# Low parts of the weights by accumulating transfers, softmax scaling on ScalarE: one decoder layer on one Trainium2 core

## The chip, the cores and the metric

The kernel runs on one NeuronCore of a Trainium2 chip. The metric is the device time of one execution in microseconds (us). The median of three runs before the change is 2506.76 us (2502.85 to 2508.31). The engines are named as in the profile: PE (TensorE, matrix multiplications), ACT (ScalarE), DVE (VectorE), POOL (GpSimd) and SP (SyncE, which issues most transfers). POOL and ACT issue transfers too. Each engine, and each of these queues, works through its instructions in order.

## What is computed

One layer of a hybrid decoder (`D_MODEL` 1024, `SEQ` 2048, 256 memory tokens, feed-forward width 2816), all in 32-bit floats:

```python
for l in range(DEPTH):                      # DEPTH = 1
    h = rmsnorm(x, mix_norm_g[l])
    proj = h @ w_in[l]
    q, k, v, g, u = jnp.split(proj, [R, 2 * R, 3 * R, 4 * R], axis=-1)
    y_ret = jax.nn.silu(g) * head_rmsnorm(retention(q, k, v, positions), ret_gn_g[l])
    y_pool = pool_mixer(u, pool_w[l], pool_scale[l])
    x = x + jnp.concatenate([y_ret, y_pool], axis=-1) @ w_out[l]
    x = x + cross_attn(rmsnorm(x, xa_norm_g[l]), mem_n, xa_wq[l], xa_wkv[l], xa_wo[l])
    x = x + conv_glu_ffn(rmsnorm(x, ffn_norm_g[l]), ffn_w_up[l], ffn_conv_w[l],
                         ffn_conv_b[l], ffn_w_down[l])
return rmsnorm(x, final_norm_g)
```

`cross_attn` takes a softmax over the 256 memory tokens for each of 4 heads.

## The kernel before

**Numbers in two parts.** Every large operand is kept as a pair: a high part, rounded to the matmul's format (`float32r`), and a low part, the rest. `passes` (L239) makes three matmuls of a product: high by high (L241), high by low (L242), low by high (L243). The pairs are made by `split` (L230): ACT copies the source into the high tile, which rounds it (L233, or L236 with a scale), and DVE subtracts that from the source (through the helper `tt`, L216; with a scale through `stt`, L225).

**Weights.** SP loads a raw weight tile of 128x1024 into one of five slots of the tile `R` (`load_tile`, L305). `pairs` splits it in two halves of 128x512, each into one of three slots of the tile `Q`, taken in turn. A slot can be written again when PE has done with the half that was in it. `unit` (L285) is one such weight tile against the 1024 tokens of a block: two halves, for each two column ranges `s` of 512 tokens, four `k` and three passes. It then hands the PSUM tile to an `evac` function. Units are used for the head inputs (three for each of 4 heads), the pool groups (4), the output projection (8, loads at L1536 and L1537) and the projection behind attention (8, from `VWd`), in each of two blocks of 1024 tokens.

**Stages.** For each block: head inputs with retention beside them; pool groups, whose halo columns `phalo` POOL copies (L630, L631); the output projection with the residual; attention; the `VWd` projection with the residual, beside which the first block loads the next block's `x` (`xT`, L524) and the second one begins the feed-forward part. The feed-forward part of both blocks follows, from about 1200 us on; it does not use `unit`. The order within an engine is laid down beforehand by a scheduler, from the program's order and its own estimate of when things are ready; nothing is reordered while it runs.

**Weight sums.** The feed-forward part needs sums of weight blocks. They are made in DRAM during the units and the attention of both blocks (`weight_sums`): SP copies four blocks (L913), and POOL issues four accumulating transfers (L915, L916, L919, L922), where L919 needs the landing of L915, and L922 that of L919. There are 34 such jobs, 136 transfers.

**Attention.** Scores for 128 tokens and two heads come from 24 matmuls. DVE takes the maximum (L871), ACT the exponentials with their sums (L875), DVE the reciprocal (L877) and the product with the exponentials (helper `ts`, L220). PE transposes the result (`turn`, L850) two tiles later. `load_m` (L835) loads and splits the folded key weights of the first two heads, then, during the first eight tiles, those of the other two.

Of the kernel before, what the change touches and what calls it, by code (L numbers as in the profile page):

```python
# [8 lines left out]
F32 = mybir.dt.float32  # L9
F32R = mybir.dt.float32r  # L10
I32 = mybir.dt.int32
AF = mybir.ActivationFunctionType
ALU = mybir.AluOpType
# [8 lines left out]
SUB = 512  # L22
# [97 lines left out]
def trunk(ctx, tc, xT, memT, pos, w_qkgu, w_v, wkv, wqT, wo, wout_r, wout_p, poolT, w_up, w_dn, vecs, consts, outT):  # L120
    nc = tc.nc
    pe, act, dve, pool, sp = nc.tensor, nc.scalar, nc.vector, nc.gpsimd, nc.sync
# [15 lines left out]
    def new_z(dtype):  # L138
        return Arena(cp.tile([P, 8 * T + 4 * EDGE], dtype, tag="Z", name=nm("Z")), 0, 8, T)
# [58 lines left out]
    def mmps():  # L198
        return mmp.tile([P, SUB], F32, tag="mm", name=nm("mm"))
# [6 lines left out]
    def aux():  # L206
        if both[0] and next(turns_) % 3 == 2:
            return single()
        return auxp.tile([P, SUB], F32, tag="aux", name=nm("aux"))

    def small(n=4):
        t = smp.tile([P, 8], F32, tag="sm", name=nm("sm"))
        return t[:, :n]

    def tt(eng, out, a, b, op):
        return eng.tensor_tensor(out=out, in0=a, in1=b, op=op)  # L216

    def ts(eng, out, a, s1, op0, s2=None, op1=None):
        if op1 is None:
            eng.tensor_scalar(out=out, in0=a, scalar1=s1, scalar2=None, op0=op0)  # L220
        else:
            eng.tensor_scalar(out=out, in0=a, scalar1=s1, scalar2=s2, op0=op0, op1=op1)

    def stt(out, a, s, b, op0=ALU.mult, op1=ALU.add):
        dve.scalar_tensor_tensor(out=out, in0=a, scalar=s, in1=b, op0=op0, op1=op1)  # L225
# [4 lines left out]
    def split(src, hi, lo, g=None):  # L230

        if g is None:
            act.activation(hi, src, AF.Copy)  # L233
            tt(dve, lo, src, hi.bitcast(F32), ALU.subtract)
        else:
            act.activation(hi, src, AF.Identity, scale=g)  # L236
            stt(lo, src, g, hi.bitcast(F32), ALU.mult, ALU.subtract)

    def passes(ps, lhs, rhs, start, stop, more=False):  # L239
        (lh, ll), (rh, rl) = lhs, rhs  # L240
        pe.matmul(ps, lh, rh, start=start, stop=False, skip_group_check=more)  # L241
        pe.matmul(ps, lh, rl, start=False, stop=False, skip_group_check=more)  # L242
        pe.matmul(ps, ll, rh, start=False, stop=stop, skip_group_check=more)  # L243

    def new_raw():
        r = raws.take()
        r.free()
        return r.f

    def new_pair():  # L250
        r = prs.take()
        r.free()
        return r.r.rearrange("p (i n) -> p i n", i=2)

    def pairs(raw):

        out = []
        for h in range(2):
            r = raw[h] if isinstance(raw, list) else raw[:, h * SUB : (h + 1) * SUB]
            pr = new_pair()  # L260
            split(r, pr[:, 0], pr[:, 1])
            out.append(pr)
        return out

# [20 lines left out]
    def unit(raw, rhs, evac, order=range(4)):  # L285


        hs = pairs(raw)
        ps = [mmps() for _ in range(NS)]
        for h in range(2):  # L290
            for s in range(NS):
                for j, kk in enumerate(order):
                    k = 4 * h + kk
                    w = [hs[h][:, i, kk * P : (kk + 1) * P] for i in range(2)]
                    passes(ps[s], w, rhs(k, s), h + j == 0, h == 1 and j == 3)
                next(behind[0], None)
                quarter[0] += 1
                if not slow[0] or quarter[0] % 2:
                    next(under[0], None)
                if h == 1:  # L300
                    evac(s, ps[s])
# [520 lines left out]
    def attention(sums, beside, pace):  # L822


        scl, nscl = (smp.tile([P, 8], F32, tag="scl", name=nm("scl"), bufs=2) for _ in range(2))
        room = B.take(2 * KT)
        third = [Region(B, room.first + KT * i, KT) for i in range(2)] + [new_z(F32R).take(KT)]
        prob = [third[1], third[0]]

        def load_m(hp):  # L830

            out = mw[hp]
            for kp in range(KT // 2):
                raw = new_raw()
                fetched[0] = sp.dma_start(raw.rearrange("p (k n) -> p k n", k=2), Md[hp, 2 * kp : 2 * kp + 2].rearrange("k p n -> p k n"))  # L835
                if hp == 0 and kp == 0:

                    out += [(pr[:, 0], pr[:, 1]) for pr in pairs(raw)]
                    yield
                    continue  # L840
                for i in range(2):
                    u = third[2 * hp].r[:, (2 * kp + i) * T : (2 * kp + i + 1) * T]
                    split(raw[:, i * SUB : (i + 1) * SUB], u[:, :SUB], u[:, SUB:])
                    out.append((u[:, :SUB], u[:, SUB:]))
                yield

        def turn(pt, t, e):
            tp = aux()
            for j in range(4):
                pe.transpose(tp[:, j * P : (j + 1) * P], e.f[:, j * P : (j + 1) * P], ident)  # L850
            pt4 = pt.r.rearrange("p (i k t) -> p i k t", i=2, t=T)[:, :, :, t * P : (t + 1) * P]
            split(tp.rearrange("p (k t) -> p k t", k=4), pt4[:, 0], pt4[:, 1])
            e.free()

        mw = [[], []]
        for _ in load_m(0):
            pass
        more_m = load_m(1)
        late = []
        for i in range(2 * KT):  # L860
            hp, t = divmod(i, KT)
            ps = mmps()
            for k in range(KT):
                x2 = [X[:, 2 * k + j, t * P : (t + 1) * P] for j in range(2)]
                passes(ps, x2, mw[hp][k], k == 0, k == KT - 1)
            if i == 0:
                rn, _, _ = norm_tables(sums, wide=False)
                ts(dve, scl, rn, 1.0 / 16.0, ALU.mult)
                ts(dve, nscl, rn, -1.0 / 16.0, ALU.mult)
            mx, sm = small(2), small(2)  # L870
            dve.reduce_max(out=mx, in_=ps.rearrange("p (h m) -> p h m", h=2), axis=AX.X)  # L871
            ts(dve, mx, mx, nscl[:, t : t + 1], ALU.mult)
            e = TT.take()
            for j in range(2):
                act.activation(e.f[:, j * NMEM : (j + 1) * NMEM], ps[:, j * NMEM : (j + 1) * NMEM], AF.Exp,  # L875
                               bias=mx[:, j : j + 1], scale=scl[:, t : t + 1], accum_out=sm[:, j : j + 1])
            dve.reciprocal(sm, sm)  # L877
            for j in range(2):
                ej = e.f[:, j * NMEM : (j + 1) * NMEM]
                ts(dve, ej, ej, sm[:, j : j + 1], ALU.mult)  # L880
            if len(late) == 2:
                turn(*late.pop(0))
            late.append((prob[hp], t, e))
            for _ in range(pace):
                next(under[0], None)
            if i < KT - 2:
                next(more_m, None)
            else:
                for _ in range(pace):
                    next(beside, None)  # L890

        def end():
            for one in late:
                yield turn(*one)

        return prob, end()
# [129 lines left out]
    class Up(Member):  # L1026
# [15 lines left out]
        def evac(self, i, ps):  # L1042
            if i == 0:
                self.gate = self.place()
            elif i == 1:
                self.val = self.place()
            which, q, how = ((0, 0, 0), (1, 1, 0), (0, 1, 0), (0, 0, 1), (1, 1, 1), (0, 1, 1), (1, 0, 0))[i]
            d = body(self.val if which else self.gate)[:, q * SUB : (q + 1) * SUB]
            if how:
                tt(dve, d, d, ps, ALU.add)  # L1050
            else:
                act.activation(d, ps, AF.Copy)
            if i > 4:
                pending.extend(self.conv(i - 5))
# [365 lines left out]
    def norm_tables(s_acc, wide=True, late=False):  # L1420

        rn = rows_norm(s_acc)
        rb, last = [], None
        if wide:
            rb = [TT.take() for _ in range(NS)]
            last = spread(rn, [r.f[:, :SUB] for r in rb], late=late)
        return rn, rb, last
# [71 lines left out]
    for b in range(NB):  # L1499
# [34 lines left out]
        for n in range(KT):  # L1534
            raw = new_raw()
# [32 lines left out]
        for n in range(KT):  # L1568
# [3 lines left out]
            def rhs(k, s):  # L1572
                at = (k % 4) * T + s * SUB
                return tuple(prob[k // 4].r[:, i * 4 * T + at : i * 4 * T + at + SUB] for i in range(2))
# [152 lines left out]
```

## Time and profile before

| | |
|---|---|
| median of three runs | 2506.76 us |
| the profiled execution | 2506.72 us |
| its span, first to last instruction | 2504.9 us |
| mean granted clock of PE | 0.992 |
| PE busy | 2442.7 us |
| DVE busy | 1666.9 us |
| ACT busy | 1216.1 us |
| POOL busy | 652.4 us |
| transfers issued by POOL | 8.9% of the 16 DMA engines' span |

How to read it: the page adds up busy time by engine. Matmuls overlap in it, so a row's mean of one matmul (some 386 ns) is longer than the time from one to the next. In the timeline, a row gives start, duration, engine, line, operation, the tile written and those read, and in brackets how long the engine had been idle and who ended that. In the groups by line, the columns are the total busy time, the mean in ns, and the idle time before with its causes. Names ending in q are an engine's queue that issues transfers.

### The profile page before, as it was taken

The numbers are of one execution on the slowest core, as the hardware profiler recorded it, in microseconds if no ns is written. First come the engines' busy times: TensorE is split into PE (matmuls) and PEld (weight loads), VectorE is DVE, ScalarE is ACT, GpSimd is POOL, SyncE is SP. The second block draws the span as 40 slices with busy tenths as digits, with TensorE's granted clock in tenths as the row PEclk, the third lists the DMA queues.
The fourth block names the chain that finished last, engine by engine and source line by source line (L and its number), as shares of the span: only waits on it lengthen the run. The fifth ranks groups of instructions, "written<-read, shape, count | busy, mean of one in ns | idle before, by whom it ended". The sixth has DMA issues, their size and how long they took to land.

```text
span 2504.9 us, 33172 instructions
## 1 busy us (share of the span) xinstructions
PE 2442.7 (98%) x11390; PEld 2037.7 (81%) x11390; DVE 1666.9 (67%) x2574; ACT 1216.1 (49%) x2163; POOL 652.4 (26%) x579
## 2 busy tenths in 40 slices
PE   6999999999999999999999999999999999999997
PEld 6888887788788888888887888878888887888885
DVE  8646566564635675574678776886677586867875
ACT  6333423343321223434654555665555576666663
POOL 1010122100121120030237352553335154222322
PEclk9999999999999999999999999999999999999998
DMA  8363888715766764366567564755556468768951
GB/s 318 89 168 110 244 191 233 234 40 181 227 152 145 159 158 149 111 221 220 167 205 270 166 203 153 236 192 165 160 160 213 136 220 287 250 185 280 346 164 68
DMA packets 257177, 474.28 MB, mean 189 GB/s; under 512 B 26864, under 2 KB 56176, under 8 KB 257008
## 3 DMA queue, kind: packets, MB, share of 16 engines
q1 hardware_dynamic: 212336, 408.18, 49.0%
q0 software_dynamic: 19584, 34.61, 8.9%
q10 hardware_dynamic: 25088, 29.37, 3.4%
q8 instruction: 89, 1.46, 0.2%
q14 instruction: 80, 0.66, 0.1%
HBM read 370.87 MB, written 170.39 MB: 216 GB/s over the span
## 4 chain that ended last, share of the span: by engine, by line
PE 78%; DMA 8%; DVE 6%; issue 3%; POOL 2%; ACT 2%; SPq 0%; POOLq 0%; ACTq 0%; DVEq 0%
PE mm L241 25%; PE mm L242 24%; PE mm L243 24%; POOL T L216 1%; DVE Z L216 1%; DMA T<-Xd 1%; DVE Z L225 1%; DVE G L216 1%; DMA T<-xT 1%; DVE Q L216 1%; DVE T L216 1%; DMA T<-Gd 1%; POOL Z L216 1%; PE aux L749 1%; DMA R<-VWd 0%
## 5 line engine op out<-in xcount | busy, mean ns | idle before, releaser
L241 PE MATMUL mm<-G,Q 128*128 128x512 f32 (+1 forms) x1888 | 728.1, 386 | 21.8 <-ACT Q L233 11.1
L243 PE MATMUL mm<-G,Q 128*128 128x512 f32 (+1 forms) x1888 | 725.9, 385 | 4.4 <-DVE Q L216 4.2
L242 PE MATMUL mm<-G,Q 128*128 128x512 f32 (+1 forms) x1888 | 725.7, 385 | 0.7 <-DVE G L216 0.7
L241 PE MATMUL mm<-G 128*128 128x512 f32 (+1 forms) x1380 | 532.1, 387 | 10.0 <-DVE Z L216 6.3
L242 PE MATMUL mm<-G 128*128 128x512 f32 (+1 forms) x1380 | 531.7, 386 | 0.0
L243 PE MATMUL mm<-G 128*128 128x512 f32 (+1 forms) x1380 | 531.1, 385 | 0.0
L241 PEld LDWEIGHTS mm<-G,Q 128*128 128x128 f32 x1888 | 357.8, 190 | 91.1 <-ACT Q L233 11.8
L243 PEld LDWEIGHTS mm<-G,Q 128*128 128x128 f32 x1888 | 357.7, 190 | 74.3 <-DVE Q L216 5.9
L242 PEld LDWEIGHTS mm<-G,Q 128*128 128x128 f32 x1888 | 358.0, 190 | 69.4 <-DVE G L216 1.6
L225 DVE SCALAR_TENSOR_TENSOR Z<-Z,vecs 128x1024 f32<-128x1024 f32 x176 | 276.3, 1572 | 153.5 <-ACT Z L1069 145.3
L241 PEld LDWEIGHTS mm<-G 128*128 128x128 f32 x1380 | 260.4, 189 | 64.5 <-DVE Z L216 8.0
L243 PEld LDWEIGHTS mm<-G 128*128 128x128 f32 x1380 | 260.2, 189 | 51.8
L242 PEld LDWEIGHTS mm<-G 128*128 128x128 f32 x1380 | 260.1, 188 | 51.5
L1006 ACT ACTIVATE G<-R 128x512 fp32r<-128x512 f32 (+1 forms) x272 | 166.5, 615 | 197.8 <-PE mm L242 178.6
L216 DVE TENSOR_TENSOR Z<-Z,mm 128x512 f32<-128x512 f32 x284 | 192.8, 679 | 78.2 <-PE mm L243 78.0
L216 DVE TENSOR_TENSOR Q<-R,Q 128x512 fp32r<-128x512 f32 x199 | 148.6, 748 | 143.4 <-ACT Q L233 138.9
L216 POOL TENSOR_TENSOR G<-R,G 128x512 fp32r<-128x512 f32 (+1 forms) x100 | 141.9, 1420 | 376.2 <-ACT G L1006 290.9
L233 ACT ACTIVATE Q<-R 128x512 fp32r<-128x512 f32 x150 | 93.8, 627 | 234.8 <-PE mm L242 187.3
L1006 ACT ACTIVATE Q<-R 128x512 fp32r<-128x512 f32 (+1 forms) x204 | 125.0, 613 | 90.9 <-PE mm L242 73.5
L216 DVE TENSOR_TENSOR G<-R,G 128x512 fp32r<-128x512 f32 (+1 forms) x168 | 131.5, 794 | 46.7 <-ACT G L233 38.0
L216 DVE TENSOR_TENSOR G<-T,G 128x512 fp32r<-128x512 f32 (+1 forms) x168 | 125.4, 758 | 53.9 <-ACT G L955 40.7
L940 ACT ACTIVATE aux<-R 128x512 f32<-128x512 f32 (+1 forms) x184 | 105.8, 576 | 95.8 <-DVE Q L216 52.9
(222 smaller groups left out, 2911.4 us busy)
## 6 DMA issues: line engine op xcount, KB each, us to landing
R<-Ud SPq DMA_DIRECT2D x176, 256.0 KB, 2.7
T<-Gd SPq DMA_DIRECT2D x168, 256.0 KB, 4.1
R<-w_up SPq DMA_DIRECT2D x132, 256.0 KB, 3.1
Gd<-Z SPq DMA_DIRECT2D x110, 256.0 KB, 2.4
Ud<-w_up SPq DMA_DIRECT2D x88, 256.0 KB, 5.9
R<-w_qkgu SPq DMA_DIRECT2D x32, 512.0 KB, 4.4
R<-Dd SPq DMA_DIRECT2D x64, 256.0 KB, 4.0
Gd<-T SPq DMA_DIRECT2D x56, 256.0 KB, 3.1
```

The lines of the kernel that those rows point to most:

```text
L216: return eng.tensor_tensor(out=out, in0=a, in1=b, op=op)
L225: dve.scalar_tensor_tensor(out=out, in0=a, scalar=s, in1=b, op0=op0, op1=op1)
L233: act.activation(hi, src, AF.Copy)
L241: pe.matmul(ps, lh, rh, start=start, stop=False, skip_group_check=more)
L242: pe.matmul(ps, lh, rl, start=False, stop=False, skip_group_check=more)
L243: pe.matmul(ps, ll, rh, start=False, stop=stop, skip_group_check=more)
L749: pe.matmul(col(self.kv, c), col(self.kn.f, c), self.ch(v, c, h * T), start=True, stop=True)
L940: act.activation(t, x, AF.Copy)
L1006: act.activation(p2[:, 0, :w], self.raw[i].f[:, :w], AF.Copy)
```

## The change

In `unit`, and for the second pair of heads in `load_m`, `split` is replaced by `moved`. ACT writes the negated source, rounded, into the low tile, and the rounded source into the high tile. A transfer issued by POOL then adds the source to the low tile. DVE takes no part. `pairs` gets the function as an argument, and its other callers keep `split`. In the softmax, the two products with the reciprocal, 128x256 each, go from DVE to ACT.

```diff
+    def moved(src, hi, lo):
+
+        act.activation(lo, src, AF.Copy, scale=-1.0)
+        act.activation(hi, src, AF.Copy)
+        pool.dma_start(lo.bitcast(F32), src, accum_op=ALU.add)
+
-    def pairs(raw):
+    def pairs(raw, how=split):
...
-            split(r, pr[:, 0], pr[:, 1])
+            how(r, pr[:, 0], pr[:, 1])
...
     def unit(raw, rhs, evac, order=range(4)):
...
-        hs = pairs(raw)
+        hs = pairs(raw, moved)
...
-                    split(raw[:, i * SUB : (i + 1) * SUB], u[:, :SUB], u[:, SUB:])
+                    (moved if hp else split)(raw[:, i * SUB : (i + 1) * SUB], u[:, :SUB], u[:, SUB:])
...
             for j in range(2):
                 ej = e.f[:, j * NMEM : (j + 1) * NMEM]
-                ts(dve, ej, ej, sm[:, j : j + 1], ALU.mult)
+                act.activation(ej, ej, AF.Identity, scale=sm[:, j : j + 1])
```

## The prediction

> **What bounds the kernel now.** I read the page first, then the waits by engine, the groups by line, the DMA issues, the busy time by stage, and last the timelines of the stages that the change touches.
>
> ```profile
> PE 2442.7 (98%) x11390; PEld 2037.7 (81%) x11390; DVE 1666.9 (67%) x2574; ACT 1216.1 (49%) x2163; POOL 652.4 (26%) x579
> q0 software_dynamic: 19584, 34.61, 8.9%
> PE 78%; DMA 8%; DVE 6%; issue 3%; POOL 2%; ACT 2%; SPq 0%; POOLq 0%; ACTq 0%; DVEq 0%
> ```
>
> PE is busy 98% of the 2504.9 us span, and it holds 78% of the chain that ended last. DVE, at 67%, has room. So work taken off DVE pays only where PE now stands idle for DVE, and a new delay costs only where it makes PE late. The busy time by stage (columns: window, PE, PEld, DVE, ACT, POOL with instruction counts, granted clock, DMA share, GB/s) gives the pace of PE and the room that is left:
>
> ```profile
> 350.00:400.00 50.00, 45.95 (x215) 37.41 (x214) 33.44 (x73) 9.43 (x22) 16.55 (x28) 1.00 0.84 183
> 600.00:650.00 50.00, 50.00 (x222) 41.42 (x221) 25.96 (x41) 19.16 (x33) 6.59 (x8) 1.00 0.76 207
> 650.00:700.00 50.00, 47.22 (x217) 39.09 (x217) 31.36 (x71) 16.94 (x30) 9.56 (x15) 0.97 0.81 249
> ```
>
> At saturation PE makes 222 matmuls in 50 us, 0.225 us each. One weight half (4 k x 2 s x 3 passes = 24 matmuls) lasts 5.4 us, a unit of two halves 10.8 us. The DMA engines are already 0.76 to 0.84 busy in these stages.
>
> **The change part by part.** The split with `moved` is made in 64 units (24 head inputs, 8 pool groups, 16 output projections, 16 `VWd` projections), two halves each, and 16 times in `load_m(1)`: 144 splits. The softmax has 64 multiplies of 128x256.
>
> ```profile
> L216 DVE TENSOR_TENSOR Q<-R,Q 128x512 fp32r<-128x512 f32 x199 | 148.6, 748 | 143.4 <-ACT Q L233 138.9 <-ACT Q L1006 3.9
> L233 ACT ACTIVATE Q<-R 128x512 fp32r<-128x512 f32 x150 | 93.8, 627 | 234.8 <-PE mm L242 187.3 <-DMA R<-w_qkgu 13.2 <-DMA R<-VWd 11.2
> L220 DVE TENSOR_SCALAR T<-T,sm 128x256 f32<-128x256 f32 x64 | 25.5, 441 | 1.0
> L236 ACT ACTIVATE G<-T,vecs 128x512 fp32r<-128x512 f32 x16 | 11.5, 719 | 28.3 <-DMA T<-xT 15.6 <-DMA Xd<-Z 12.7
> ```
>
> DVE loses 144 x 0.748 = 108 us and 25.5 us of multiplies. ACT gains 144 x 0.627 = 90 us for the negated copies, and the multiplies: a scale taken from a column costs 0.719 - 0.627 = 0.09 us more than a copy of the same size, so a 128x256 one lies between half of 0.719 (0.36) and the whole, I take 0.5, 32 us in all. By totals alone both fit: in the three windows above ACT is busy 9 to 19 of 50 us.
>
> The transfers are the new thing. The nearest rows are the 136 accumulating transfers of the weight sums, issued by the same POOL queue, 256 KB like the new ones (some 192 KB), but from DRAM to DRAM. The four lines of the sums, asked one by one, end with these answers:
>
> ```profile
> L919 POOL DMA_DIRECT2D Ud<-Ud x22: 806/812/1112, 56.3 to 705.9; - x22
> DMA to landing us min/median/max: 3.7/5.9/9.6
> DMA to landing us min/median/max: 3.8/6.4/10.4
> DMA to landing us min/median/max: 3.7/4.8/8.8
> DMA to landing us min/median/max: 3.7/5.3/7.4
> ```
>
> An issue takes 0.81 us of POOL (144 x 0.81 = 117 us, which POOL has), and from its start to the landing 3.7 to 10.4 us pass; I take 5.5, the middle of the four medians. SBUF to SBUF could be nearer 3.7, a busier set of engines nearer 7; both ends are kept. The DMA engines pay 8.9% x 2504.9 / 136 = 1.6 us each for one such transfer; two per 10.8 us unit add 0.30 to shares that now read 0.76 to 0.84, so back-to-back units would ask for slightly more than there is.
>
> The path of a half is now: slot free, ACT copies 0.63, hand-over 0.1, POOL and transfer 5.5, so 6.2 us after ACT begins, against about 1.7 now (start to end of the DVE step). Three pair slots in turn leave two halves, 10.8 us, and the low part is first read by the third matmul of its half, 0.45 us later. The spare is 10.8 + 0.45 - 6.2 = 5.0 us, where ACT begins as soon as PE frees the slot (187.3 of ACT's 234.8 us idle before these copies ended so). Where is that cover gone? I found four places, (a) to (d).
>
> (a) *`VWd` of the first block.* Here ACT begins a half not when the slot is free but behind its own waits for `xT`:
>
> ```profile
> 645.59 0.62 ACT L233 ACTIVATE Q<-R 128x512 fp32r<-128x512 f32 x1
> 646.60 0.68 DVE L216 TENSOR_TENSOR Q<-R,Q 128x512 fp32r<-128x512 f32 x1
> 576.16 0.48 PE L241 MATMUL mm<-G,Q 128*128 128x512 f32 x1
> 647.34 0.39 PE L241 MATMUL mm<-G,Q 128*128 128x512 f32 x1
> 618.89 0.68 DVE L216 TENSOR_TENSOR Q<-R,Q 128x512 fp32r<-128x512 f32 x1
> 619.60 0.33 SPq L305 DMA_DIRECT2D R<-w_qkgu  x1
> 623.47 0.48 SPq L524 DMA_DIRECT2D T<-xT  x1
> ```
>
> The stage's matmuls begin at 576.16; counted from there, the one at 647.34 opens the fourteenth half. Its low part ended on DVE at 647.28, half a us before the third matmul. By the new path it lands at 645.59 + 6.2 = 651.8: 4.0 us late. This is a shift of the stage, to be paid about once, not per half. Second, the raw tile is held until the transfer has landed. The load at 619.60 went out as the DVE step at 618.89 ended (619.57); now it waits some 4.6 us longer, and behind it in SP's order stand the sums' loads and the `xT` tile of 623.47, on which ACT's next halves wait. For some four units that is up to 15 us, less where the order of the queue differs or the cover takes it; I take 4. Together 8, ends 0 and 19.
>
> (b) *`VWd` of the second block.*
>
> ```profile
> 1140.90 0.62 ACT L233 ACTIVATE Q<-R 128x512 fp32r<-128x512 f32 x1
> 1146.45 0.39 PE L241 MATMUL mm<-G,Q 128*128 128x512 f32 x1
> 1146.23 0.10 POOL L1617 MEMSET Z<- 128x2 f32 x1 [7.97 <-DMA Xd<-Z]
> ```
>
> The half begun at 1140.90 is read from 1146.9 on. It would land at 1147.1, just late, and at 1151.8 if its transfer stands behind the memset for which POOL waited 7.97 us. I take 3, ends 0 and 8.
>
> (c) *Pool groups and the start of the output projection.* POOL works in order, and its waits are seen to reach PE already:
>
> ```profile
> 383.98 0.81 POOL L919 DMA_DIRECT2D Ud<-Ud  x1 [5.65 <-DMA Ud<-w_up]
> 384.51 0.48 POOL L630 COPY T<-phalo 128x16 f32<-128x16 f32 x1
> 385.03 0.71 DVE L216 TENSOR_TENSOR T<-T 128x527 f32<-128x527 f32 x1 [8.86 <-POOL T L630]
> 392.52 0.73 PE L241 MATMUL mm<-G,Q 128*128 128x512 f32 x2 [3.00 <-ACT G L233]
> ```
>
> A 16-column copy stood behind a sum's wait of 5.65 us, DVE stood 8.86 us for the copy, and PE 3.00 us at the end. Each pool unit now puts two more issues, 1.6 us, in front of such copies, and each issue waits for ACT; a new transfer behind a wait of 5.65 us overruns its spare of 5.0 by 0.6. On the other side DVE's backlog shrinks. I take +4 over both blocks, ends -3 (that idle gone) and +15.
>
> (d) *Head inputs with sums running.*
>
> ```profile
> POOL Ud L922 <- DMA Ud<-Ud: 90.9, 19, 7.8
> POOL Ud L919 <- DMA Ud<-w_up: 84.6, 18, 7.9
> ```
>
> A mean wait is 4.7 us, just inside the spare; the longest, 7.8, overruns it by 2.8. A single such overrun makes +2, ends 0 and 6. Once the last sum is issued this is over, and the rest of the second output projection costs nothing under the 5.0 us spare. `load_m(1)` is needed eight tiles later and costs nothing.
>
> (e) *Attention.* The start of the first one is a stop that the change loosens:
>
> ```profile
> 494.33 0.63 ACT L233 ACTIVATE Q<-R 128x512 fp32r<-128x512 f32 x1 [11.22 <-DMA R<-VWd]
> 494.99 0.69 DVE L216 TENSOR_TENSOR Q<-R,Q 128x512 fp32r<-128x512 f32 x1 [7.90 <-ACT Q L233]
> 499.12 0.56 ACT L875 ACTIVATE T<-mm,sm,scl 128x256 f32<-128x256 f32 x1
> 500.96 1.11 PE L850 MATMUL aux<-consts,T 128*128 128x128 f32 x4 [4.34 <-DVE T L220]
> ```
>
> DVE's early split waited 7.90 us for ACT, with the norm's steps behind it. Without it they are done before 494.33, and ACT's first exponential moves from 499.12 to about 497, gain 2. The multiplies on ACT stand behind the next tile's exponentials, two of 0.56, loss about 1 at the start; later the transposes come two tiles on, 10.8 us, which hides 1.0 us of ACT per tile. Net -1, ends -4 and +3.
>
> The sum is 8 + 3 + 4 + 2 - 1 = +16. The profiled execution took 2506.72 us (span 2504.9 and 1.8 around it), 0.04 us from the median of 2506.76, so the forecast is 2506.7 + 16 = 2523 us. The feed-forward part after about 1200 us is untouched.
>
> **The rivals.**
>
> *Faster: DVE's relief decides.* PE's two long stops shown, 4.34 and 3.00 us, both lie behind DVE. If the transfers land in about 3.7 us and stand ahead of the sums' waits, they are covered nearly everywhere, and both stops go: 2506.7 - 7.3 = 2499. For it speaks the 7.90 us wait in (e); against it that the fourteenth half in (a) is 2.2 us late even at 3.7. It decides when landings stay at the low end in the `VWd` stages and ACT reaches its halves there 2 us sooner, DVE being freer. Chance 0.17.
>
> *Hidden: no change.* With landings at the low end of 3.7, (a) is 2.2, (b) and (d) nothing, (c) nothing where copies stand ahead, (e) -2: 2507. The Trainium skill, "DMA: Bandwidth & Descriptors", Anatomy of one DMA, gives about 2.0 us plus bytes over 436e3 for a transfer from GpSimd, for 256 KB an estimate of 2.6 us; by that figure the fourteenth half would be 1.1 us late, with (e) the sum is about 2506. None of the 136 transfers shown landed in under 3.7. Chance 0.13.
>
> *Much slower: POOL's order decides.* If the new transfers land 7 us after issue and half of some 60 halves stand behind a mean wait of 4.7, each is 4.7 + 7 + 0.73 - 11.25 = 1.2 us late and delays the next sum in turn: 30 x 1.2 = 36, with the +16 about 2559. For it speaks a DMA share that would pass 1.0; against it that sums pause for long stretches. Chance 0.12.
>
> **How the numbers follow.** The forecast has 0.58. Measurement can tell about 0.2%, 5 us. Slower: 0.58 + 0.12 = 0.70; the same: 0.13; faster: 0.17. The terms' ends are not met together; the range 2500 to 2555 takes in the hidden case, the edge of the faster one and most of the slow one.
>
> **What would show it.** Right: `Q<-R` gone from DVE, PE idle before L243 with a transfer into `Q` as releaser, most of it near 630 to 670 and 1130 to 1165 us; POOL copies of `phalo` later; first exponentials of attention earlier; landings of 4 to 7 us. Wrong: no idle of PE behind those transfers, or landings under 3.5 us; or PE idle spread over the head inputs, which is the POOL rival.

## The result, and the profile after

The changed kernel takes 2635.9 us (median of five runs, 2632.66 to 2640.01) against 2507.5 us of the kernel before (median of five, 2502.85 to 2508.36): a ratio of 1.052, 95% interval 1.050 to 1.054, slower by some 128 us. The forecast of 2523 had the sign and missed the size by 113 us, and the range ended at 2555. The profiled execution took 2635.9 us, its span 2634.1.

The page of the changed kernel: busy time of the engines, and POOL's queue (17.4% of the DMA engines' span, 8.9% before).

```profile
PE 2479.4 (94%) x11390; PEld 2060.1 (78%) x11390; DVE 1557.7 (59%) x2366; ACT 1314.6 (50%) x2369; POOL 777.9 (30%) x723
q0 software_dynamic: 40320, 72.37, 17.4%
```

DVE lost 109 us and ACT gained 98; 134 and 122 had been taken. No engine became the bound. Two other numbers moved: PE's share fell from 98 to 94%, and its busy time rose by 36.7 us although it makes the same 11390 matmuls. The groups and the waits say which matmuls wait, and for what (in the waits: total us, count, longest). First the group of the changed kernel:

```profile
L243 PE MATMUL mm<-G,Q 128*128 128x512 f32 (+1 forms) x1888 | 739.4, 393 | 90.7 <-DMA Q<-R 86.0
```

The same row of the kernel before:

```profile
L243 PE MATMUL mm<-G,Q 128*128 128x512 f32 (+1 forms) x1888 | 725.9, 385 | 4.4 <-DVE Q L216 4.2
```

The waits of the changed kernel:

```profile
PE mm L243 <- DMA Q<-R: 86.0, 22, 12.0
POOL Ud L921 <- DMA Ud<-w_up: 156.2, 19, 32.1
POOL Ud L928 <- DMA Ud<-Ud: 78.8, 16, 7.8
POOL Ud L925 <- DMA Ud<-w_up: 61.0, 16, 7.1
```

(Lines behind L255 have moved by six: the pass that reads the low part is still L243, the low copy is L257, the new transfer L259, and the four transfers of the sums are L921, L922, L925 and L928. In `traffic_only` L244 is the first of the three passes, in `placed_sums` L245 the last.) PE waited 22 times for a new transfer, 86 us in all, up to 12 us at a time; before, the idle time in front of this line was 4.4 us. And POOL waited at its sums: at L921 for SP's copies, at L925 and L928 for the sum before. (These three rows are those that write `Ud`, 22 jobs; the 12 jobs that write `Dd` have rows of their own, 89.1 us at L921, 25.0 at L925 and 38.9 at L928.)

By stage (columns as in the prediction), the loss is where the prediction's term (c) stands, far above its price:

```profile
350.00:400.00 50.00, 39.30 (x174) 32.59 (x173) 22.16 (x57) 11.47 (x32) 15.86 (x24) 0.86 0.86 167
400.00:450.00 50.00, 35.30 (x136) 27.61 (x135) 21.69 (x37) 13.08 (x23) 15.35 (x22) 0.86 0.84 187
1000.00:1050.00 50.00, 41.03 (x208) 34.75 (x208) 24.04 (x59) 11.01 (x31) 14.04 (x21) 0.88 0.76 161
1100.00:1150.00 50.00, 50.00 (x226) 41.52 (x225) 22.49 (x35) 25.45 (x46) 8.80 (x11) 1.00 0.74 203
```

PE makes 136 matmuls in 50 us where it can make 222, and the granted clock falls to 0.86. After the last sum has been issued, at 1057 us, PE is full again (226 matmuls in the last window), with the same transfers under way. One stop of PE, followed back in the timeline of the changed kernel:

```profile
979.33 0.61 ACT L257 ACTIVATE Q<-R 128x512 fp32r<-128x512 f32 x1
985.31 0.81 POOL L928 DMA_DIRECT2D Dd<-Dd  x1 [4.54 <-DMA Dd<-Dd]
985.84 1.20 POOL L259 DMA_DIRECT2D Q<-R  x1
995.19 0.83 POOL L921 DMA_DIRECT2D Dd<-w_dn  x1 [8.15 <-DMA Dd<-w_dn]
997.29 0.84 POOL L922 DMA_DIRECT2D Dd<-w_dn  x1 [1.27 <-DMA Dd<-w_dn]
997.83 1.23 POOL L259 DMA_DIRECT2D Q<-R  x1
1004.99 0.79 PE L243 MATMUL mm<-G,Q 128*128 128x512 f32 x1 [7.74 <-DMA Q<-R]
```

The half's low copy was done on ACT at 979.94. Its transfer went out at 997.83, 17.9 us later. In front of it in POOL's queue stood one wait for a landing (4.54 us), the transfer of the half before it, one wait for SP's copy (8.15) and one more (1.27). From issue to landing another 7.1 us passed. Over all halves, from the end of ACT's low copy to the issue: the median is 8.2 us among the 15 halves begun from 350 to 480 us and 8.3 among the 28 from 790 to 1060, the longest 17.6 and 18.4, and 0.36 elsewhere. The prediction's spare was 5.0. Put side by side with the stops: 14 of the 22 stops, 68 of the 86 us, were for a half whose transfer went out over 7 and up to 18.4 us after its low copy. Another 13 us lie in the two `VWd` stages and at the start of the second block; there it went out 0.35 to 2.5 us after.

The sum of the difference: PE's stops of over 0.25 us grew from 52.4 to 145.4 us, 93 more. Its busy time grew by 36.7 us; the clock was at half for 119.5 us in place of 17.1 (from 40 to 2450 us), in part while PE stood. Together 129.7, and the spans differ by 129.2.

### The profile page after: what moved, and what is told of

Read it like the earlier page. It is cut to its first block, busy times and chain, and to the rows that moved or that the text cites. A ratio compares the mean times of both kernels' runs of the same rounds, so it can differ in the third digit from the quotient of the medians.

```text
span 2634.1 us, 33497 instructions
## 1 busy us (share of the span) xinstructions
PE 2479.4 (94%) x11390; PEld 2060.1 (78%) x11390; DVE 1557.7 (59%) x2366; ACT 1314.6 (50%) x2369; POOL 777.9 (30%) x723
## 3 DMA queue, kind: packets, MB, share of 16 engines
q0 software_dynamic: 40320, 72.37, 17.4%
## 4 chain that ended last, share of the span: by engine, by line
PE 49%; DMA 6%; DVE 3%; issue 2%; POOL 2%; ACT 1%; SPq 0%; POOLq 0%; DVEq 0%; ACTq 0%
PE mm L243 16%; PE mm L241 16%; PE mm L242 16%; DMA T<-Gd 2%; DMA Q<-R 1%; DVE G L216 1%; DVE Z L216 1%; DMA T<-Xd 1%; DVE Z L225 1%; POOL T L216 1%; DMA outT<-T 1%; DMA Dd<-w_dn 1%; POOL Z L216 1%; DMA Dd<-Dd 0%; DMA T<-Hd 0%
## 5 line engine op out<-in xcount | busy, mean ns | idle before, releaser
L243 PE MATMUL mm<-G,Q 128*128 128x512 f32 (+1 forms) x1888 | 739.4, 393 | 90.7 <-DMA Q<-R 86.0
L241 PE MATMUL mm<-G,Q 128*128 128x512 f32 (+1 forms) x1888 | 738.5, 392 | 20.0 <-ACT Q L233 11.1
L242 PE MATMUL mm<-G,Q 128*128 128x512 f32 (+1 forms) x1888 | 734.7, 389 | 0.0
L243 PE MATMUL mm<-G 128*128 128x512 f32 (+1 forms) x1380 | 530.7, 385 | 0.0
L243 PEld LDWEIGHTS mm<-G,Q 128*128 128x128 f32 x1888 | 364.5, 193 | 172.0 <-DMA Q<-R 96.7
L241 PEld LDWEIGHTS mm<-G,Q 128*128 128x128 f32 x1888 | 364.9, 193 | 90.4 <-ACT Q L233 11.8
L242 PEld LDWEIGHTS mm<-G,Q 128*128 128x128 f32 x1888 | 364.6, 193 | 70.4 <-DVE G L216 0.4
L243 PEld LDWEIGHTS mm<-G 128*128 128x128 f32 x1380 | 260.0, 188 | 51.8
L259 POOL DMA_DIRECT2D Q<-R x128 | 129.4, 1046 | 453.8 <-ACT Q L257 438.8
L258 ACT ACTIVATE Q<-R 128x512 fp32r<-128x512 f32 x128 | 80.5, 629 | 206.7 <-PE mm L242 161.9
```

The source lines that it names most:

```text
L259: pool.dma_start(lo.bitcast(F32), src, accum_op=ALU.add)
```

## The experiments

Theory 1: the sums' waits in POOL's queue hold the new transfers up. Against it stand theories in which the transfers would be late anyhow: by their own length, or by the traffic of the sums on the DMA engines and in the queue behind the issue (theory 2, or the rival). Theory 3 puts the loss on ACT's extra work. Ratios are to the kernel before, with 95% intervals.

### The two parts of the change, one by one

Kernel before with this edit alone (`softmax_alone`), and the change without it (`moved_alone`):

```diff
-                ts(dve, ej, ej, sm[:, j : j + 1], ALU.mult)
+                act.activation(ej, ej, AF.Identity, scale=sm[:, j : j + 1])
```

> Only the softmax's multiplies go to ScalarE; all splits stay on VectorE. Theory 1 (POOL's order: the new transfers stand behind the weight sums' waits) and theory 2 (the transfers themselves: their landing and the load of the DMA engines) both put nothing of the loss here: 2505 to 2512 us. Theory 3 (ScalarE: its extra copies and multiplies make it late) expects a visible part of the 128 us, 2520 us or more.

> Only the accumulating transfers, the softmax stays on VectorE. Theories 1 and 2: the whole loss, 2625 to 2645 us. Theory 3: clearly less than the whole change, under 2620 us.

Measured: the softmax alone 2504.1 us, ratio 0.999 [0.998, 1.000]; the transfers alone 2636.2 us, 1.052 [1.050, 1.054]. All of the loss belongs to the transfers. The multiplies gain 1 us by the medians and 2.5 by the ratio, and zero is not excluded.

### The sums taken out, in both kernels

Both kernels leave out POOL's four transfers of each job, so the feed-forward part gets only the copied blocks:

```diff
-            pool.dma_start(d[2], a22, accum_op=ALU.add, max_dma_last_dim=2048)
-            pool.dma_start(d[0], a21, accum_op=ALU.add, max_dma_last_dim=2048)
...
-            pool.dma_start(d[1], d[2], accum_op=ALU.add, max_dma_last_dim=2048)
...
-            pool.dma_start(d[3], d[1], accum_op=ALU.add, max_dma_last_dim=2048)
```

> The kernel before without the four accumulating transfers of each weight sum (SyncE's copies of the weight blocks stay, so the sums are not the true ones). It is the base for the next run. All theories: TensorE does not wait for the sums, so 2495 to 2508 us; a few us less than before, as POOL's halo copies no longer stand behind them.

> The whole change, without the accumulating transfers of the weight sums. POOL's queue then holds nothing that waits long, while all 144 new transfers and their landings stay. Theory 1 (POOL's order): at most 20 us over the base without sums, what is left lying in the VWd stages: 2505 to 2525 us, and from the end of the low copy to the issue 0.4 us at the median everywhere. Theory 2 (the transfers' landing and DMA load): a loss of half the 128 us or more stays, 2565 us or more.

Measured: 2495.5 us, 0.996 [0.995, 0.998], and 2521.8 us, 1.007 [1.005, 1.008]. Without the sums the change costs 1.03%, 26 us, in place of 128. The group of the changed kernel without sums:

```profile
L243 PE MATMUL mm<-G,Q 128*128 128x512 f32 (+1 forms) x1888 | 726.9, 386 | 18.3 <-DMA Q<-R 13.6 <-DVE Q L216 4.6
```

PE's idle time behind the transfers falls from 86.0 to 13.6 us, and its matmuls take 386 ns again. So four fifths of the loss go with the sums. This doesn't yet say whether by their waits or by their traffic.

### The chain of the sums cut (`unchained`)

The third and fourth transfer of a job add blocks of the weights, which need no landing (the sums are then not the true ones):

```diff
-            pool.dma_start(d[1], d[2], accum_op=ALU.add, max_dma_last_dim=2048)
+            pool.dma_start(d[1], a22, accum_op=ALU.add, max_dma_last_dim=2048)
-            pool.dma_start(d[3], d[1], accum_op=ALU.add, max_dma_last_dim=2048)
+            pool.dma_start(d[3], a21, accum_op=ALU.add, max_dma_last_dim=2048)
```

> The whole change, but the third and fourth accumulating transfer of each weight sum add a weight block of the same size instead of the result of the earlier ones, so that POOL no longer waits for landings in the middle of a sum (the sums are then not the true ones). Transfers, bytes and issues are as many as in the change. Theory 1: most waits in front of the new transfers go, from the end of ScalarE's low copy to the issue under 3 us in the median of the stages with sums, and the time falls to 2525 to 2570 us. Theory 2: the DMA load is the same, so 2615 to 2640 us.

Measured: 2605.0 us, 1.040 [1.038, 1.042], which neither theory had expected: only 31 us came back. The waits of this kernel:

```profile
PE mm L243 <- DMA Q<-R: 67.4, 18, 9.4
POOL Ud L921 <- DMA Ud<-w_up: 207.1, 19, 32.4
```

The waits of L925 and L928 were gone, but that of L921 for SP's copies grew from 156 to 207 us: POOL came to it sooner and waited there instead. Among the halves from 790 to 1060 us the median from low copy to issue fell from 8.3 to 0.36 us, but the longest was still 15.1; and the landings became longer (median 6.6 in place of 5.6), with four sums in the queue together. By its total the run mixes both theories. By its halves it speaks for theory 1: of the 67 us that PE waited, 49 were for halves whose transfer still went out 5 to 15 us after the low copy. Of the sums' waits, only those for SP's copies were left to hold them; how these come to stand there time after time is shown with step (c) below.

### The traffic without the need for it (`traffic_only`)

DVE makes the low parts as before; POOL issues as many plain copies of the raw halves to a spare area in DRAM:

```diff
-        act.activation(lo, src, AF.Copy, scale=-1.0)
-        act.activation(hi, src, AF.Copy)
-        pool.dma_start(lo.bitcast(F32), src, accum_op=ALU.add)
+        split(src, hi, lo)
+        pool.dma_start(Sd[next(spare)], src)
```

> Softmax as in the change. VectorE makes the low parts as before, and POOL issues as many transfers of the same raw halves at the same places, to DRAM places of their own that nothing reads (an addition: plain copies, not accumulating). The load of POOL's queue and of the DMA engines is there, and raw slots are held as long, but TensorE waits for no transfer. Theory 1: 2507 to 2535 us, what is over 2507 by raw slots held behind POOL's waits. Theory 2: if the load of the DMA engines is what costs, 2560 us or more.

Measured: 2528.3 us, 1.009 [1.007, 1.011]. So 144 more transfers in POOL's queue, which no matmul needs, cost 24 us. One stop makes up half of it:

```profile
412.57 1.22 PE L244 MATMUL mm<-G,Q 128*128 128x512 f32 x2 [11.82 <-ACT G L236]
```

It stands in the pool groups, behind ACT and not behind a transfer into `Q`. ACT had waited 16.75 us for DVE, and DVE for one of POOL's copies of `phalo` (in this kernel L638; the sum in front of it is L930):

```profile
407.85 0.84 POOL L930 DMA_DIRECT2D Ud<-Ud  x1 [6.71 <-DMA Ud<-Ud]
408.39 0.50 POOL L638 COPY T<-phalo 128x16 f32<-128x16 f32 x1
408.93 0.71 DVE L219 TENSOR_TENSOR T<-T 128x527 f32<-128x527 f32 x1 [11.07 <-POOL T L638]
```

So this half of the 24 us comes by a step that stands behind a sum's wait in POOL's queue, as in (c) of the prediction. What the added traffic did to that wait (5.65 us at such a place before) can't be told apart.

### Another maker of the low parts (`pool_subtract`)

```diff
-        act.activation(lo, src, AF.Copy, scale=-1.0)
         act.activation(hi, src, AF.Copy)
-        pool.dma_start(lo.bitcast(F32), src, accum_op=ALU.add)
+        tt(pool, lo, src, hi.bitcast(F32), ALU.subtract)
```

> As the change, but in place of the transfer POOL itself subtracts the high part from the source (128x512, about 1.4 us), in the same places of the same queue; the sums stay. The position behind the sums' waits remains, the landing of 3.3 to 10 us is gone. Theory 1: the delays in front of POOL's step remain several us in the stages with sums, and since a half then has 4 us more to spare, 2520 to 2560 us. Theory 2: nothing of the cost is left, 2500 to 2512 us.

Measured: 2542.1 us, 1.015 [1.013, 1.017]. The wait of its matmuls:

```profile
PE mm L243 <- POOL Q L216: 15.2, 6, 4.4
```

The same place in POOL's queue, without the 5 us of a landing: PE waits 15.2 us in all in place of 86. Two things have part in it: no landing follows, and POOL comes to its step sooner. From the end of ACT's high copy to POOL's step the median is 5.9 us from 350 to 480 us and 2.8 from 790 to 1060 (8.2 and 8.3 in the change), the longest 14.7. How much each is worth was not tried.

### The transfers only behind attention (`vwd_only`)

`moved` in the 32 halves of `VWd` alone, `split` elsewhere, the multiplies on ACT (`unit` gets the function as an argument; of the edit, the call is shown):

```diff
-            unit(load_tile(VWd[n]), rhs, add_residual(b, n, xs, acc=acc[n]))
+            unit(load_tile(VWd[n]), rhs, add_residual(b, n, xs, acc=acc[n]), how=moved)
```

> The accumulating transfers only in the VWd projections of both blocks (32 of 144), the softmax on ScalarE; all other splits on VectorE. It prices the two terms of the prediction that were put there, 8 and 3 us. Theory 1 (POOL's order, sums nearly absent in these stages): 2507 to 2522 us. Theory 2 (landings and held raw slots): 2530 us or more.

Measured: 2517.9 us, 1.006 [1.004, 1.007], 12.4 us over the median beside it. From the timeline of PE and ACT in this kernel:

```profile
626.48 0.50 PE L243 MATMUL mm<-G,Q 128*128 128x512 f32 x1 [1.30 <-DMA Q<-R]
635.92 0.50 PE L243 MATMUL mm<-G,Q 128*128 128x512 f32 x1 [3.69 <-DMA Q<-R]
652.61 0.50 PE L243 MATMUL mm<-G,Q 128*128 128x512 f32 x1 [3.27 <-DMA Q<-R]
1152.20 0.80 PE L243 MATMUL mm<-G,Q 128*128 128x512 f32 x1 [2.46 <-DMA Q<-R]
636.62 0.72 ACT L236 ACTIVATE G<-T,vecs 128x512 fp32r<-128x512 f32 x1 [11.29 <-DMA T<-xT]
```

Three stops in the first block, 8.3 us, and one in the second, 2.5: terms (a) and (b), taken at 8 and 3. ACT does wait longer for `xT` (11.29 us once; the prediction's row of L236 has 15.6 us for all such waits together).

### The copies of `phalo` moved to DVE (`halo_dve`, `halo_softmax`, `halo_after`)

```diff
-            pool.tensor_copy(u.f[:, 0:16], phalo[:, g])
-            pool.tensor_copy(phalo[:, g], u.f[:, SUB : SUB + 16])
+            dve.tensor_copy(u.f[:, 0:16], phalo[:, g])
+            dve.tensor_copy(phalo[:, g], u.f[:, SUB : SUB + 16])
```

> The kernel before, with the two 16-column copies of phalo (L630, L631) on DVE instead of POOL; splits, softmax and sums as before. Theory 1 (POOL's order is what delays others, already in the kernel before): the stop of PE near 392 us, which went back through DVE to a copy standing behind a sum's wait, goes; the program without the sums gained 9 to 10 us, and the copies are its part in the pool groups: 2497 to 2503 us. Rival (the sums cost by their traffic on the DMA engines, not by the order): the stop moves to another cause and the time stays at 2504 to 2509.

> As halo_dve, with the softmax's multiplies on ACT as well, the part of the change that alone gave about -2 us. Theory 1: the two gains add up: 2495 to 2502 us, below both kernels. Rival: 2503 to 2507, no better than the softmax alone (2504).

> The change, with the two 16-column copies of phalo on DVE instead of POOL. Theory 1 (the new transfers themselves stand behind the sums' waits and PE waits for them): little is won, since those transfers stay where they were: 2605 to 2636 us, PE's idle time behind the transfers into Q still over 70 us. Rival (in the pool groups the loss comes by the copies, which make DVE, and PE with it, late): the loss of that stage in the first block, some 33 us of idle time and its share of the half clock, mostly goes: 2560 to 2600.

Measured: in the kernel before, 2499.3 us, 0.997 [0.996, 0.998]; with the softmax's multiplies on ACT too, 2497.1 us, 0.9973 [0.9963, 0.9982]; in the changed kernel, 2634.8 us, 1.052 [1.050, 1.053]. Where the pool groups stopped for 3.00 us before, the window of `halo_softmax` is full, and the start of attention no longer stops:

```profile
350.00:400.00 50.00, 50.00 (x239) 41.86 (x238) 37.16 (x85) 11.01 (x24) 11.72 (x14) 1.00 0.90 212
```

```profile
L850 PE MATMUL aux<-consts,T 128*128 128x128 f32 x128 | 19.5, 272 | 0.0
```

This version is faster than both kernels, by 0.27%. It shows theory 1 in the kernel before on a small scale: two copies of 16 columns taken out from behind the waits of the sums were worth 5.6 us. The stop at the start of attention is gone in `halo_dve` as well (its idle time there is 0.0), so the two edits share this gain, and the multiplies add at most a little. In the changed kernel the move brings nothing; the wait is the transfers' own:

```profile
PE mm L243 <- DMA Q<-R: 83.3, 22, 14.0
```

### The transfers where POOL's queue runs empty (`wout_second`)

`moved` only in the 16 halves of the second block's output projection, and the multiplies on ACT (again only the call is shown):

```diff
-            unit(raw, ..., add_residual(b, n, xs, got=got), (0, 2, 3, 1))
+            unit(raw, ..., add_residual(b, n, xs, got=got), (0, 2, 3, 1), moved if b else split)
```

> The accumulating transfers only in the 16 halves of the second block's output projection, of which the later ones run when the last sum has been issued; all other halves split on DVE; softmax on ACT. Theory 1 (a transfer costs nothing where POOL's queue is empty): PE loses at the first one or two halves, under 5 us, and nothing behind, so 2503 to 2511 us, with landings of 3.3 to 4.5 us. Rival (each transfer is late by its own length, wherever it stands): 16 halves at 1 to 3 us each, 2520 to 2550.

Measured: 2515.5 us (2510.83 to 2526.11), 1.005 [1.003, 1.006], above theory 1's 2511 and under the rival's 2520. In the profiled execution (2522.9 us) one half of 16 made PE wait long. The timeline of POOL, ACT and PE around it:

```profile
930.62 0.64 ACT L257 ACTIVATE Q<-R 128x512 fp32r<-128x512 f32 x1
941.89 0.82 POOL L925 DMA_DIRECT2D Dd<-Dd  x1 [6.30 <-DMA Dd<-w_dn]
942.46 1.17 POOL L259 DMA_DIRECT2D Q<-R  x1
947.89 0.80 PE L243 MATMUL mm<-G,Q 128*128 128x512 f32 x1 [10.93 <-DMA Q<-R]
```

The third half's transfer went out 11.2 us after its low copy, behind the last job's L921 (issued at 933.68) and the wait of 6.30 us at its L925, and PE stood 10.93 us for it. The last sum went out at 946.92. From there on 13 halves follow each other at PE's pace, each issued 0.35 to 0.49 us after its low copy and landed 3.3 to 6.0 us later, and the first of them cost 0.50 us, the others nothing. This is the case in small: the same transfer, with and without a wait in front of it, in one stage. What was wrong in the expectation is the price of one overrun, set at under 5 us, and the landings, set at 4.5 us at most.

### The traffic without the waits (`unwaited`, `placed_sums`), and the waits without the traffic (`small_sums`)

In `unwaited` each of the 136 sums adds a block of the weights to an area of its own; in `placed_sums` it is besides queued behind the newest transfer into `Q`; in `small_sums` it keeps its waits and moves 8 of 128 rows:

```diff
-            pool.dma_start(d[1], d[2], accum_op=ALU.add, max_dma_last_dim=2048)
# unwaited
+            pool.dma_start(e[2], a22, accum_op=ALU.add, max_dma_last_dim=2048)
# placed_sums
+            with tc.issue_after(latest[0].ins):
+                pool.dma_start(Ad[at + 2][:, : a22.shape[-1]], a22, accum_op=ALU.add, max_dma_last_dim=2048)
# small_sums
+            pool.dma_start(d[1][0:8], d[2][0:8], accum_op=ALU.add, max_dma_last_dim=2048)
```

> The change, with the sums' 136 accumulating transfers kept in number, size and place in the program, but each adding a block of the weights to an area of its own that nothing else writes or reads; so none waits for a copy of SP or for another transfer. The feed-forward part gets only the copied blocks. Theory 1 (the waits in POOL's order hold the new transfers): they are gone, the traffic stays, so the loss falls to what the change cost without the sums, 26 us, plus 10 to 20 for transfers that land later: 2530 to 2560 us, and the time from ACT's low copy to the issue is about 0.4 us nearly everywhere. Rival (the sums' traffic, on the DMA engines and in POOL's ring, is what makes the new transfers late): 2600 to 2640 us.

> The change, with each of the sums' 136 accumulating transfers cut to 8 of 128 rows, a sixteenth of the bytes; their order and all their waits (for SP's copies, and for one another's landings) stay. The sums are true only in these rows. Theory 1: the waits for SP's copies stay and the chain's waits shorten to 2 or 3 us, so much of the loss stays: 2560 to 2610 us. Rival (traffic): the loss falls to what the change cost without the sums: 2520 to 2540 us.

> As unwaited (136 accumulating transfers of the same size, each into an area of its own, without any wait), but each queued behind the last transfer into Q that the program has issued before it, so that they stay spread over the stages of both blocks as in the change. Without that order unwaited sent all of them in the first 240 us and lost its time there. Theory 1 (the sums' waits in POOL's order): with the waits gone the time from ACT's low copy to the issue is about 0.4 us in all stages, PE's idle time behind the transfers into Q falls from 86 to under 30 us, and the program takes 2530 to 2565 us. Rival (the sums' traffic makes the new transfers land late, whatever the order): landings of 6 to 8 us in the stages with sums, idle time still over 55 us, 2590 to 2640 us.

`unwaited` took 2628.8 us, 1.050 [1.048, 1.051]. The number lies in the rival's 2600 to 2640, but says nothing on the question. With no wait to hold them, all 136 transfers were issued in the first 240 us, the first at 1.25 us, and POOL's own arithmetic of the program's start stood among them, for which PE waited 56.4 us:

```profile
L322 PE MATMUL aux<-consts,T 128*128 128x1 f32 x116 | 14.5, 247 | 56.4 <-POOL T L217 56.4
```

`small_sums` took 2542.8 us, 1.016 [1.014, 1.017], between the two expectations. Its waits:

```profile
PE mm L243 <- DMA Q<-R: 29.0, 14, 4.5
POOL Ud L928 <- DMA Ud<-Ud: 37.0, 14, 7.9
POOL Ud L921 <- DMA Ud<-w_up: 148.2, 18, 31.6
```

The waits for SP's copies mostly stayed (218 us in all, with those of `Dd`, in place of 245), those of the chain fell by more than half, because a wait in the chain is the landing of the sum before. So this run took away traffic and part of the waits together. It also shows that the waits for SP's copies alone don't make the loss.

`placed_sums` took 2555.9 us, 1.021 [1.019, 1.023], within theory 1's 2530 to 2565 and far under the rival's 2590. POOL has no wait at a sum left, but for issuing, and PE waits 34.4 us in all:

```profile
POOL Ad L918 <- issue: 11.6, 9, 1.8
PE mm L245 <- DMA Q<-R: 34.4, 13, 9.6
```

(34.4 is above the 30 that theory 1 had allowed.) The median from low copy to issue is 0.35 or 0.36 us in every stage. Of the 34.4 us, 22 are in the stages with sums; the rest is in and right behind the `VWd` projections. What is left of the sums' part is traffic. The same window in this kernel and in the one without sums, first `placed_sums`:

```profile
400.00:450.00 50.00, 40.86 (x168) 32.73 (x168) 17.80 (x27) 19.56 (x35) 18.16 (x21) 0.95 1.05 266
```

```profile
400.00:450.00 50.00, 50.00 (x222) 41.42 (x221) 19.57 (x30) 21.48 (x38) 7.88 (x10) 1.00 0.84 229
```

With the sums' traffic the DMA engines' share is 1.05 (0.84 without), and the two transfers in this stretch that made PE wait landed 13.4 and 12.8 us after issue.

**The account in per cent of before.** The change without sums 1.0066 - 0.9963 = 1.03, some 26 us. The sums' traffic under it, `placed_sums` against `no_sums_after`, 1.39, some 35 us. The sums' waits, the change against `placed_sums`, 3.14, some 79 us. From this goes what the sums cost in the kernel before, 0.37, some 9 us. Together 5.19, the measured loss, as the four differences must. The split between waits and traffic rests on one kernel, `placed_sums`, whose sums lie near, not at, the places of the change. `unchained` and `small_sums` don't give such a split, since a wait in the chain is itself the landing of a sum: less traffic also means shorter waits.

## Why the prediction failed in its size

**Held.** (a) and (b): 11 us, measured 12.4 with 10.7 of idle time in the stages named (12.7 in the changed kernel, with one stop of 2.33 at the start of the next stage). The way was different, and that the sums agree is in part luck: in (a) not one late half, the fourteenth, but the tenth, eleventh and thirteenth, whose transfers landed 5.5 to 9.7 us after issue; in (b) a landing of 7.3 us, with no memset in front of the transfer. (d) in the first block: no stop behind a transfer before 350 us, though two stops behind ACT (L750), 2.36 and 3.50 us, are new there. The pause after the last sum: 0.4 us of stops in the rest of the second output projection. The landings of 5.5 us: median 5.7 from this answer for L259 of the changed kernel,

```profile
DMA to landing us min/median/max: 3.2/5.7/15.7
```

and none under 3.2: the estimate of 2.6 us that the prediction worked out from the Trainium skill's figure ("DMA: Bandwidth & Descriptors", Anatomy of one DMA) isn't borne out here.

**(c) is the step that failed, and with it (d) in the second block.** They were taken at 4 and 2 us, with upper ends of 15 and 6. The runs give 102 us for what goes with the sums. Three errors lie in that step. First, "a new transfer behind a wait of 5.65 us overruns its spare of 5.0 by 0.6" sets one wait in front of a transfer. POOL's queue held two or three, the waits for SP's copies (156 and 89 us in all) among them, which the prediction's terms left out: it looked at L922 and L919 only. The spare was smaller too, by some 0.8 us: on ACT the high copy comes first (0.54 us from its start to that of the low one), and from the low copy to the issue 0.35 us pass at least, in place of 0.1. The view of the kernel before that has those two rows has these as well:

```profile
POOL Ud L915 <- DMA Ud<-w_up: 384.8, 16, 109.8
POOL Dd L915 <- DMA Dd<-w_dn: 85.1, 11, 27.6
```

Second, the delay feeds itself, through SP. A raw tile is free only when the new transfer has read it. SP's next load waits for that (at L1542 SP waits 124 us in all for landings into `Q`; before, 60 us there for DVE's subtractions), SP's copies for the next sum stand behind this load in SP's order, and POOL waits for the copies in front of the next new transfer. One turn of this in the changed kernel, which began as a new transfer had landed, at 393.90:

```profile
393.95 0.34 SPq L1542 DMA_DIRECT2D R<-wout_r  x1
401.98 2.42 SPq L919 DMA_DIRECT2D Ud<-w_up  x4
405.88 0.83 POOL L921 DMA_DIRECT2D Ud<-w_up  x1 [8.44 <-DMA Ud<-w_up]
406.44 1.18 POOL L259 DMA_DIRECT2D Q<-R  x1
413.17 0.75 PE L243 MATMUL mm<-G,Q 128*128 128x512 f32 x1 [4.95 <-DMA Q<-R]
```

(Between the first two, SP waited for the landing of one more such transfer, at 401.56.) From 350 to 480 us SP's loads for the output projection waited 76 us for landings into `Q`. From 373 to 432 us stops of 5 to 8 us come some 20 us apart, one for each job of the sums, where before there was one of 3.00 us. `unchained` left this circle whole: SP's copies for two jobs follow there at 396.98 and 417.53. Part (a) of the prediction has the held raw tile and the sums' loads behind it, but only for the `VWd` stage. No run broke the circle alone. Third, no price stood for the clock: 36.7 us of slower matmuls.

**(e)** The start of attention was to gain 2 us. Alone, the softmax's edit took that stop from 4.34 to 0.82 us, but in the changed kernel it is 4.70 us, now behind ACT (`<-ACT T L886`): the multiplies stand behind a low copy for which ACT waits 8.52 us, until its raw tile of `VWd` is loaded. Without the sums the stop is 4.79 us, so they are not its cause. No gain, within the ends kept.

**The signs named.** PE's idle time has the transfer into `Q` as its releaser, as said, but it was to lie near 630 to 670 and 1130 to 1165 us. By far the most of it, 73 of 86 us, lies from 370 to 480 and from 880 to 1060: 28 us in the pool groups, 34 in the output projections, 11 in the second block's head inputs.

**The rival "POOL's order decides"** named the cause, and had a chance of 0.12 and 52 us (its 2559 lay above the range's end of 2555, though the range was said to take in most of it). Its 1.2 us for each late half is what failed: it took half of 60 halves at one mean wait. In fact 22 halves made PE wait, 3.9 us each on average, and the clock's part came on top. "Against it that sums pause for long stretches" was true of the wrong stretches: they do not pause in the pool groups.

## What to carry to other kernels

Before a step that is on the path of the bound goes into a queue that works in order, list every wait that already stands in that queue in those stages, with its longest, and add two or three of them up before comparing with the spare. Ask also whether what is waited for there waits, by another queue, for the new step itself. A transfer is a poor stand-in for a 0.75 us vector step where its landing alone, 5.7 us, takes half of the cover. The same look, taken the other way, gave the only gain here: two small copies moved out of that queue, 5.6 us.

## What the hardware showed beyond that

**A short stop costs twice.** Stops of 2.32, 2.36, 2.38 and 2.51 us were each enough for a spell at half clock; stops of 2.33, 2.95 and 3.28 weren't. The length alone doesn't decide. In the changed kernel all changes of the granted clock lie on one grid of 3.41 us, and the spells are 3.4, 6.8, 10.2 and 13.7 us long. What counts is how much of a stop falls into one window of that grid. The stop of 2.38 us, from 677.40 to 679.78, and then the one of 2.33, from 729.25 to 731.58, each with its two windows:

```profile
676.08:679.49 3.41, 1.32 (x6) 0.75 (x4) 2.17 (x4) 1.60 (x3) 0.63 (x1) 1.00 1.11 195
679.49:682.90 3.41, 3.12 (x7) 2.48 (x8) 0.00 (x0) 0.00 (x0) 1.09 (x2) 0.50 1.13 237
```

```profile
727.28:730.69 3.41, 1.97 (x9) 1.31 (x7) 1.20 (x2) 1.96 (x4) 0.00 (x0) 1.00 1.07 334
730.69:734.11 3.42, 2.53 (x12) 2.10 (x13) 2.83 (x6) 2.56 (x6) 0.70 (x2) 1.00 0.33 87
```

The first stop leaves PE 1.32 us of one window, and the next window is at 0.50. The second falls on the border of two windows, and both keep the full clock. From 60 to 2450 us of this trace, each window at full clock in which PE stood for some 2.1 us or more is followed by half clock (20 of them), and none in which it stood for 1.87 or less; in other traces a few windows with less idle time were followed too. The Trainium skill, "TensorE: Matmul & The Clock Gate", What's actually happening, has half clock after an idle window of about 3.4 us; the grid agrees with such a window, but here a window idle for 2.1 of 3.41 us brought it about.

**An accumulating transfer into SBUF** of 256 KB landed in 3.2 us at best, in 5.7 at the median of the change, and in 12.8 and 13.4 us where the DMA engines' share read 1.05 (`placed_sums`).
